# Down projection: the next chunk's weight loads queued behind the fifth product's token operands, and a 384-byte filler in phase one

## The chip, the cores and the metric

The kernel runs on one core of one Trainium2 chip. A core has TensorE (PE in the profile, with PEld for its weight loads), VectorE (DVE), ScalarE (ACT), GpSimd (POOL) and SyncE (SP), which here issues nearly all DMA transfers. Each engine runs its own instruction list in order. The metric is the device time of one execution in microseconds (us).

## The reference

A trunk of two layers on 1024 tokens of width 1024, in float32. Each layer computes

```
h = rms_norm(x, attn_norm[l])
proj = h @ w_in[l]                  # 1312 columns, shared by three mixers
mixed = concat(sliding-window attention, pooling mixer, latent attention)
x = x + mixed @ w_out[l]
h = rms_norm(x, ffn_norm[l])
x = x + (silu(h @ w_gate[l]) * (h @ w_up[l])) @ w_down[l]    # width 2816
```

The change concerns the last product of the last line, and the memory layout of the first product.

## The kernel before

Every float32 product is made of three TensorE passes: each operand is split into a rounded part and a remainder (`split`, line 58: a ScalarE copy, then a VectorE subtraction), and the passes are high by high, high by low and low by high.

A layer has these parts. **Phase one** (`phase1`) makes the input projection, the windowed attention and the pooling mixer, 128 tokens at a time. **Phase two** (`phase2`) makes the latent attention and the output projection. `gate_up` makes the gate and up products and their gated product; `down` makes the down projection.

Both feed-forward halves use a seven-product scheme for 2 by 2 blocks (Winograd's form of Strassen's), so each block product takes seven multiplications and a number of additions. `gate_up` works on eleven column pairs. For each pair its generator `operands` forms seven combinations of the gated product, splits each of them and stores the two parts in DRAM, in `gd[i][0]` to `gd[i][6]` (line 1278). The stores of the last pair are left to the generator in `G["kept"]`, which `down` drives on.

**The down projection.** The eleven pairs are taken in four chunks of 2, 3, 3 and 3 pairs. For a chunk of h pairs, `load` (line 1026) brings 2h blocks of `w_down`, 512 KB each, into a tile `rw`. Chunk one has a buffer of its own; chunks two, three and four use the pool `even`, which has two buffers, so that chunk four takes the one that chunk two had. `chunk` then makes seven products in the order 1, 2, 5, 6, 3, 7, 4. For each product, `operands(at, p, b)` does two things:

- it loads the token operand, h transfers of 512 KB from `gd` into a tile `ga` (line 1041); the pool `sg` has four `ga` buffers, so the operand of the fifth product can be loaded only when the first product is done;
- it splits the weight operand `q[b]` into a tile `op` (ACT line 1043, DVE line 1044); the pool `sw` has three buffers. Between them `sub` (POOL line 1034) forms sums of weights in place in `rw`.

Each product then takes four groups of 3h matmuls (lines 1085 to 1087), one group for each 128 token rows, with a sum in PSUM (`acc`), which ACT (line 1090) or DVE (`add`, line 1075) moves to the accumulators `a1`, `a5`, `a6` and `xrow`. In chunk one, `rows` reloads the residual rows `xrow` from DRAM (line 1050) and drives `G["kept"]`.

**What sets the order.** The text gives priorities; a scheduler then fixes each engine's instruction list before the run, by simulating a timeline: among the instructions that are ready in that simulation it takes the one that stands earlier in the text. On the chip the lists are run as they are, and every instruction waits for the semaphores of its inputs and of the buffers that it overwrites. `tc.issue_after(ins)` places what is traced in its block behind `ins` on the same engine's list; it adds no wait for `ins` to end.

In the text, the loads of the next chunk (`ahead()`) stand behind the third product's operands.

**Phase one's layout.** Pools take SBUF in the order in which they are opened. `gap` opens a pool that only takes room, and writes one element of it on POOL (line 52) so that the pool exists. Two such gaps, of 1024 and 2176 bytes for each partition, stand in `phase1`. The pools `wt` (the first 512 columns of the projection's weights, `wa`) and `wz` (a part of the other columns, `wb`) are the last ones.

Of the kernel before, what the change touches and what calls it, by code (L numbers as in the profile page):

```python
# [21 lines left out]
P = 128  # L22
# [14 lines left out]
def trunk(ctx: ExitStack, tc: tile.TileContext, A, out):  # L37
# [62 lines left out]
    for l in range(DEPTH):  # L100
        xsrc = A["x"][0] if l == 0 else xres
        G = dict(
            ident=ident, xm=xm, xrow=xrow, krr=krr, rc=rc, cosT=cosT, sinT=sinT, sinks=sinks,
            pscale=pscale, invc=invc, nhalf=nhalf, gq=gq, gm=gm, cmask=cmask, identr=identr, rn=rn, gc=gc, g32=g32, xsrc=xsrc, dram=dram, gap=gap, xp=xp, gns=ExitStack(), bias_keep=bias_keep)
        G["gna"], G["gains"], G["gqk"] = gna, gains, gqk
        phase1(nc, tc, A, l, pool, split, f, bcast, G)
        phase2(nc, tc, A, l, pool, split, f, bcast, G)
        phase34(nc, tc, A, l, pool, split, f, bcast, G, xres, out)
# [217 lines left out]
def phase1(nc, tc, A, l, pool, split, f, bcast, G):  # L326
    ve, sc, gp, te, sy = nc.vector, nc.scalar, nc.gpsimd, nc.tensor, nc.sync
    cosT, sinT = G["cosT"], G["sinT"]
    ident, xm, xrow, krr = G["ident"], G["xm"], G["xrow"], G["krr"]
    with ExitStack() as ph:  # L330
        gap = G["gap"]
# [14 lines left out]
        hp = [pool(ph, f"p1h_{l}"), hq]  # L346
        early = pool(ph, f"p1e_{l}")
        wj = pool(ph, f"p1j_{l}")
        wt = pool(ph, f"p1t_{l}")
        wz = pool(ph, f"p1z_{l}")  # L350
        ps_mm = pool(ph, f"p1mm_{l}", bufs=2, space=PSUM)
# [21 lines left out]
        hTs, rows = {}, {}  # L373
        behind = []
        ahead = {}
# [60 lines left out]
        for t in range(NT):  # L436
# [3 lines left out]
            hT, r = hTs[t], rows[t]  # L440
# [149 lines left out]
            for g in range(2):  # L590
# [3 lines left out]
                for i0, ni in ((0, 2), (2, 1)):  # L594
                    s = ps_sc.tile([P, 2, 256], F32, name="s")
                    for i in range(i0, i0 + ni):
                        h = 3 * g + i
# [6 lines left out]
                for i in range(3):  # L604
                    h = 3 * g + i
# [3 lines left out]
                for i in range(3):  # L609
                    h = 3 * g + i  # L610
# [373 lines left out]
def phase34(nc, tc, A, l, pool, split, f, bcast, G, xres, out):  # L984
    ve, sc, gp, te, sy = nc.vector, nc.scalar, nc.gpsimd, nc.tensor, nc.sync
    ident, xm, xrow, xp = G["ident"], G["xm"], G["xrow"], G["xp"][l]
    last = l == DEPTH - 1
    HB = S // 2
    HK = KT // 2
    gd = [[G["dram"].tile([P, 2, HB], F32, name=f"gd{l}_{i}_{p}") for p in range(7)] for i in range(NF // 2)]  # L990

    with ExitStack() as ph:
        ps_gu = pool(ph, f"p4gu_{l}", bufs=5, space=PSUM)
        ps_d = pool(ph, f"p4dn_{l}", bufs=3, space=PSUM)
        gate_up(nc, tc, A, l, pool, split, f, bcast, G, ps_gu, ps_d, gd)
        G["gns"].close()

        down(nc, tc, A, l, pool, split, f, G, (ps_gu, ps_d), gd, xres, out)


def down(nc, tc, A, l, pool, split, f, G, banks, gd, xres, out):

    ve, sc, gp, te, sy = nc.vector, nc.scalar, nc.gpsimd, nc.tensor, nc.sync
    xrow, xp = G["xrow"], G["xp"][l]
    last = l == DEPTH - 1
    LEFT, RIGHT = slice(0, 512), slice(512, 1024)
    with ExitStack() as ph:  # L1010
        sg = pool(ph, f"p5s_{l}", bufs=4)
        ac = pool(ph, f"p5a_{l}")
        a1 = ac.tile([P, 4, 512], F32, name="a1")
        a5 = ac.tile([P, 4, 512], F32, name="a5")
        a6 = ac.tile([P, 4, 512], F32, name="a6")
        even = pool(ph, f"p5e_{l}", bufs=2)
        G["go"] = pool(ph, f"p5g_{l}", bufs=2)
        sw = pool(ph, f"p5w_{l}", bufs=3, side="right")

        def load(ps, rp):  # L1020
            h = len(ps)
            rw = rp.tile([P, 2 * h, D], F32, name="rw")
            for b in range(2):
                for j, i in enumerate(ps):
                    r = (2 * i + b) * P
                    sy.dma_start(rw[:, b * h + j], A["w_down"][l, r : r + P, :])
            q = {f"B{a + 1}{b + 1}": rw[:, a * h : a * h + h, c] for a in range(2) for b, c in enumerate((LEFT, RIGHT))}
            return ps, q, h

        def chunk(loaded, first, final, ahead=None):  # L1030
            ps, q, h = loaded

            def sub(o, a, b):
                gp.tensor_tensor(out=o, in0=a, in1=b, op=ALU.subtract)  # L1034

            ops, nxt = {}, []

            def operands(at, p, b):
                ga = sg.tile([P, 3, 2, 512], F32R, name="ga")
                for j, i in enumerate(ps):  # L1040
                    sy.dma_start(f(ga[:, j]), gd[i][at])
                t = sw.tile([P, 2, 3, 512], F32R, name="op")[:, :, 0:h]
                sc.copy(t[:, 0], q[b])  # L1043
                ve.tensor_tensor(out=t[:, 1], in0=q[b], in1=f(t[:, 0]), op=ALU.subtract)  # L1044
                ops[p] = ga, t

            def rows(ts, n):
                if first:
                    for t in ts:
                        sy.dma_start(xrow[t], xp[t])  # L1050
                    for _ in range(n):
                        next(G["kept"], None)

            operands(0, 1, "B11")
            operands(1, 2, "B21")
            rows(range(4), 0)
            sub(q["B12"], q["B12"], q["B11"])
            operands(2, 5, "B12")
            rows(range(4, 6), 7)
            if ahead is not None:  # L1060
                nxt.append(ahead())
            sub(q["B12"], q["B22"], q["B12"])
            operands(3, 6, "B12")
            rows(range(6, 8), 0)
            if first:
                for t in range(4, NT):
                    gp.tensor_tensor(out=xrow[t][:, LEFT], in0=xrow[t][:, LEFT], in1=xrow[t][:, RIGHT], op=ALU.subtract)
            sub(q["B11"], q["B12"], q["B11"])
            sub(q["B21"], q["B21"], q["B12"])
            operands(4, 3, "B22")  # L1070
            operands(5, 7, "B11")
            operands(6, 4, "B21")

            def add(o, a, eng=ve):
                eng.tensor_tensor(out=o, in0=o, in1=a, op=ALU.add)

            for at, p in enumerate((1, 2, 5, 6, 3, 7, 4)):
                S_, T_ = ops[p]
                for i in range(4):
                    lo, hi = xrow[i], xrow[i + 4]  # L1080
                    n = 4 * at + i
                    acc = banks[n % 8 > 4].tile([P, 512], F32, name="dn", tag=("gu", "dn")[n % 8 > 4])
                    ts = slice(i * P, (i + 1) * P)
                    for j in range(h):
                        te.matmul(acc, S_[:, j, 0, ts], T_[:, 0, j], start=j == 0, stop=False)  # L1085
                        te.matmul(acc, S_[:, j, 0, ts], T_[:, 1, j], start=False, stop=False)  # L1086
                        te.matmul(acc, S_[:, j, 1, ts], T_[:, 0, j], start=False, stop=j == h - 1)  # L1087
                    dst = (a1[:, i], lo[:, LEFT], lo[:, RIGHT], hi[:, LEFT], a5[:, i], a6[:, i], hi[:, RIGHT])[p - 1]
                    if first and p in (1, 5, 6):
                        sc.copy(dst, acc)  # L1090
                    else:
                        add(dst, acc)
                    if not final:
                        continue
                    if p == 1:
                        add(lo[:, LEFT], a1[:, i], gp)
                    elif p == 6:
                        add(a6[:, i], a1[:, i], gp)
                        add(hi[:, LEFT], a6[:, i], gp)
                        add(a5[:, i], a6[:, i], ve)  # L1100
                        add(lo[:, RIGHT], a5[:, i], ve)
                    elif p == 7:
                        add(hi[:, LEFT], hi[:, RIGHT], ve)
                        add(hi[:, RIGHT], a5[:, i], ve)
                    if p in (3, 4):
                        t = i if p == 3 else i + 4
                        dst = out[0] if last else xres
                        sy.dma_start(dst[t * P : (t + 1) * P, :], xrow[t])
            return nxt

        with ExitStack() as st:
            first = load(range(0, 2), pool(st, f"p5z_{l}", side="right"))
            nxt = chunk(first, True, False, lambda: load(range(2, 5), even))
        nxt = chunk(nxt[0], False, False, lambda: load(range(5, 8), even))
        nxt = chunk(nxt[0], False, False, lambda: load(range(8, 11), even))
        chunk(nxt[0], False, True)


# [271 lines left out]
```

## Time and profile before

| | |
|---|---|
| median of 3 runs | 2178.31 us (2177.22 to 2181.81) |
| profiled execution | 2177.97 us |
| its span, first to last instruction | 2176.1 us |
| mean granted TensorE clock | 0.990 |
| down projection, layer 0, on PE | 874.4 to about 1091 us |
| down projection, layer 1, on PE | 1956.1 to about 2171 us |

Times in the views are in us from the span's start. A row of the timeline gives the start, the length, the engine, the line, the operation, the tiles as output<-input, and the count; what stands in brackets is how long the engine was idle before it, and what released it. On SP a row counts issues of transfers, whose data land later. In a view of stretches, `PE busy (x)` is the busy time and the number of instructions that lie in the stretch, PEclk is the clock that was granted, DMA share the share of the sixteen DMA engines' time, and GB/s what they moved.

### The profile page before, as it was taken

Reading aid. Unit: us, or ns where it says so; the run is one execution under the profiler, and the core shown is the slowest. Engines: PE = TensorE matmul, PEld = TensorE weight load, DVE = VectorE, ACT = ScalarE, POOL = GpSimd, SP = SyncE. Lnnn points to the kernel's source line nnn. Section 1 sums busy time; section 2 is a strip of 40 time slices with the busy share of each in tenths; the row PEclk is TensorE's granted clock in tenths of the full one; section 3 lists DMA queues with packets and bytes.
Section 4 is the critical chain, followed back from the end, with each engine's and each line's share of the span. In section 5 each row is a group of like instructions: output and inputs, shape, how many; then the busy total and the mean of one; then the engine's idle time right before and its main releaser. Section 6 shows DMA issues by size and latency. Waiting matters only on the chain.

```text
span 2176.1 us, 29696 instructions
## 1 busy us (share of the span) xinstructions
PE 2096.3 (96%) x10423; PEld 1756.8 (81%) x10423; DVE 1689.1 (78%) x2595; ACT 1084.4 (50%) x2301; POOL 976.0 (45%) x916
## 2 busy tenths in 40 slices
PE   8998999999999999999989989999999999999999
PEld 6886898877888888788878868888778888887887
DVE  6567888799888887765756678887998878877657
ACT  7777676663434333321267777766534443333111
POOL 2445456256544452522624354552654545436215
PEclk9999999999999999999999999999999999999999
DMA  7002211324445335975530122113144344369754
GB/s 232 1 1 97 92 45 49 117 87 145 164 144 176 136 136 194 411 300 196 204 105 1 37 93 83 49 59 128 69 158 169 138 156 151 140 229 406 272 200 164
DMA packets 133732, 312.16 MB, mean 143 GB/s; under 512 B 13071, under 2 KB 63952, under 8 KB 133584
## 3 DMA queue, kind: packets, MB, share of 16 engines
q1 hardware_dynamic: 133396, 310.19, 39.8%
q8 instruction: 83, 1.36, 0.2%
q14 instruction: 65, 0.53, 0.1%
q10 hardware_dynamic: 188, 0.08, 0.0%
HBM read 203.53 MB, written 106.70 MB: 143 GB/s over the span
## 4 chain that ended last, share of the span: by engine, by line
PE 45%; DVE 7%; DMA 5%; issue 2%; ACT 2%; POOL 1%; SPq 0%; DVEq 0%; ACTq 0%; POOLq 0%
PE dn L1085 5%; PE dn L1086 5%; PE dn L1087 5%; PE gu L1240 5%; PE gu L1239 5%; PE gu L1238 5%; PE acc L446 2%; PE acc L447 2%; PE acc L448 2%; DMA ga<-gd 1%; DMA rw<-in_w_down_dram 1%; PE tp L847 1%; PE po L888 1%; PE po L886 1%; PE po L887 1%
## 5 line engine op out<-in xcount | busy, mean ns | idle before, releaser
L1240 PE MATMUL gu<-T,sb 128*128 128x512 f32 x704 | 274.8, 391 | 9.0 <-DVE sb L58 8.8
L1238 PE MATMUL gu<-T,sb 128*128 128x512 f32 x704 | 274.9, 390 | 4.9 <-DVE B L58 2.0
L1239 PE MATMUL gu<-T,sb 128*128 128x512 f32 x704 | 274.0, 389 | 0.0
L1085 PE MATMUL dn<-op,ga 128*128 128x512 f32 x616 | 240.6, 392 | 8.5 <-DMA ga<-gd 8.5
L1086 PE MATMUL dn<-op,ga 128*128 128x512 f32 x616 | 240.7, 391 | 0.0
L1087 PE MATMUL dn<-op,ga 128*128 128x512 f32 x616 | 239.9, 391 | 0.0
L58 ACT CAST go<-xm 128x512 fp32r<-128x512 f32 x154 | 94.8, 620 | 264.5 <-POOL xm L1272 98.6
L1034 POOL TENSOR_TENSOR rw<-rw 128x1536 f32<-128x1536 f32 (+1 forms) x32 | 110.9, 3477 | 245.3 <-DVE op L1044 156.3
L1043 ACT CAST op<-rw 128x1536 fp32r<-128x1536 f32 (+1 forms) x56 | 76.9, 1376 | 284.9 <-PE dn L1087 266.6
L1215 POOL TENSOR_TENSOR xm<-raw 128x512 f32<-128x512 f32 x44 | 68.1, 1550 | 322.3 <-DMA raw<-in_w_up_dram 110.5
L58 DVE TENSOR_TENSOR go<-xm,go 128x512 fp32r<-128x512 f32 x154 | 155.8, 1021 | 34.2 <-ACT go L58 30.1
L58 ACT CAST sb<-raw 128x512 fp32r<-128x512 f32 x180 | 110.1, 617 | 118.0 <-PE gu L1240 97.2
L1240 PEld LDWEIGHTS gu<-T,sb 128*128 128x128 f32 x704 | 132.1, 188 | 40.4 <-DVE sb L58 13.1
L1238 PEld LDWEIGHTS gu<-T,sb 128*128 128x128 f32 x704 | 132.1, 188 | 35.2 <-ACT sb L58 3.5
L58 DVE TENSOR_TENSOR sb<-raw,sb 128x512 fp32r<-128x512 f32 x180 | 157.2, 874 | 1.3 <-ACT sb L58 0.3
L1272 POOL TENSOR_TENSOR xm<-xm 128x512 f32<-128x512 f32 x88 | 142.6, 1628 | 30.1 <-DVE go L58 19.3
L1239 PEld LDWEIGHTS gu<-T,sb 128*128 128x128 f32 x704 | 132.2, 188 | 27.2
L1044 DVE TENSOR_TENSOR op<-rw,op 128x1536 fp32r<-128x1536 f32 (+1 forms) x56 | 114.4, 2044 | 39.1 <-ACT op L1043 36.1
L1085 PEld LDWEIGHTS dn<-op,ga 128*128 128x128 f32 x616 | 116.4, 189 | 34.5 <-issue 7.3
L1087 PEld LDWEIGHTS dn<-op,ga 128*128 128x128 f32 x616 | 116.2, 189 | 24.6
L1086 PEld LDWEIGHTS dn<-op,ga 128*128 128x128 f32 x616 | 116.5, 189 | 24.0
L1238 PE MATMUL gu<-B,A 128*128 128x512 f32 x336 | 131.5, 391 | 2.8 <-ACT B L58 2.8
(332 smaller groups left out, 6071.4 us busy)
## 6 DMA issues: line engine op xcount, KB each, us to landing
gd<-go SPq DMA_DIRECT2D x154, 512.0 KB, 3.1
ga<-gd SPq DMA_DIRECT2D x154, 512.0 KB, 5.9
raw<-in_w_gate_dram SPq DMA_DIRECT2D x22, 1024.0 KB, 5.6
raw<-in_w_up_dram SPq DMA_DIRECT2D x22, 1024.0 KB, 6.2
rw<-in_w_down_dram SPq DMA_DIRECT2D x44, 512.0 KB, 8.7
xp<-stage SPq DMA_DIRECT2D x32, 256.0 KB, 2.0
old<-xp SPq DMA_DIRECT2D x16, 512.0 KB, 4.2
xp<-xm SPq DMA_DIRECT2D x16, 512.0 KB, 2.9
```

Source lines behind the costliest of these rows:

```text
L58: return sc.copy(hi, src), ve.tensor_tensor(out=lo, in0=src, in1=f(hi), op=ALU.subtract)
L1034: gp.tensor_tensor(out=o, in0=a, in1=b, op=ALU.subtract)
L1043: sc.copy(t[:, 0], q[b])
L1044: ve.tensor_tensor(out=t[:, 1], in0=q[b], in1=f(t[:, 0]), op=ALU.subtract)
L1085: te.matmul(acc, S_[:, j, 0, ts], T_[:, 0, j], start=j == 0, stop=False)
L1086: te.matmul(acc, S_[:, j, 0, ts], T_[:, 1, j], start=False, stop=False)
L1087: te.matmul(acc, S_[:, j, 1, ts], T_[:, 0, j], start=False, stop=j == h - 1)
L1215: gp.tensor_tensor(out=s1, in0=q["A21"], in1=q["A22"], op=ALU.add)
L1238: te.matmul(acc, s[:, 0, k], b[:, 0, k], start=k == 0, stop=False)
L1239: te.matmul(acc, s[:, 0, k], b[:, 1, k], start=False, stop=False)
L1240: te.matmul(acc, s[:, 1, k], b[:, 0, k], start=False, stop=k == HK - 1)
L1272: gp.tensor_tensor(out=q[o], in0=q[a], in1=q[b], op=op)
```

## The change

The loads of a chunk get a `pin`: an earlier issue on SP behind which they are queued, one behind the other. `operands` keeps its last `ga` transfer in `pin`. The loads for the next chunk move in the text from behind the third product's operands (`operands(2, 5, ...)`) to behind those of the fifth (`operands(4, 3, ...)`), and are pinned to the last of that operand's transfers. The step `rows(range(4, 6), 7)`, which loads two residual rows and drives the seven kept stores, moves behind the fourth product's operands. This holds for the first three chunks; the fourth has nothing to load ahead. In `phase1`, a third gap of 384 bytes stands ahead of `wt`.

```diff
+        gap(ph, f"p1m_{l}", 384)
         wt = pool(ph, f"p1t_{l}")
         wz = pool(ph, f"p1z_{l}")
...
-        def load(ps, rp):
+        def load(ps, rp, pin=None):
             h = len(ps)
             rw = rp.tile([P, 2 * h, D], F32, name="rw")
             for b in range(2):
                 for j, i in enumerate(ps):
                     r = (2 * i + b) * P
-                    sy.dma_start(rw[:, b * h + j], A["w_down"][l, r : r + P, :])
+                    with tc.issue_after(pin.ins) if pin else nullcontext():
+                        pin = sy.dma_start(rw[:, b * h + j], A["w_down"][l, r : r + P, :])
...
             ops, nxt = {}, []
+            pin = []
 
             def operands(at, p, b):
                 ga = sg.tile([P, 3, 2, 512], F32R, name="ga")
                 for j, i in enumerate(ps):
-                    sy.dma_start(f(ga[:, j]), gd[i][at])
+                    pin[:] = [sy.dma_start(f(ga[:, j]), gd[i][at])]
...
             operands(2, 5, "B12")
-            rows(range(4, 6), 7)
-            if ahead is not None:
-                nxt.append(ahead())
             sub(q["B12"], q["B22"], q["B12"])
             operands(3, 6, "B12")
+            rows(range(4, 6), 7)
             rows(range(6, 8), 0)
...
             operands(4, 3, "B22")
+            if ahead is not None:
+                nxt.append(ahead(pin[0]))
             operands(5, 7, "B11")
...
-            nxt = chunk(first, True, False, lambda: load(range(2, 5), even))
-        nxt = chunk(nxt[0], False, False, lambda: load(range(5, 8), even))
-        nxt = chunk(nxt[0], False, False, lambda: load(range(8, 11), even))
+            nxt = chunk(first, True, False, lambda pin: load(range(2, 5), even, pin))
+        nxt = chunk(nxt[0], False, False, lambda pin: load(range(5, 8), even, pin))
+        nxt = chunk(nxt[0], False, False, lambda pin: load(range(8, 11), even, pin))
```

## The prediction, made before the changed kernel had run

> **What bounds the kernel now.** I read the page's head first, then stretches of the down projection, then TensorE's waits, then its timeline and SP's.
>
> ```profile
> PE 2096.3 (96%) x10423; PEld 1756.8 (81%) x10423; DVE 1689.1 (78%) x2595; ACT 1084.4 (50%) x2301; POOL 976.0 (45%) x916
> ```
>
> TensorE is busy for 2096.3 of 2176.1 us. Time can be won only where PE waits or runs at a lower clock; a faster helper elsewhere wins nothing.
>
> ```profile
> 874.00:919.00 45.00, 40.24 (x170) 32.32 (x169) 35.81 (x30) 16.54 (x24) 26.31 (x11) 0.96 1.03 411
> 1956.00:2001.00 45.00, 41.29 (x174) 33.34 (x174) 33.83 (x27) 17.59 (x25) 25.70 (x11) 0.96 1.02 410
> 919.00:1091.00 172.00, 171.93 (x759) 142.04 (x757) 114.18 (x130) 36.60 (x32) 62.95 (x26) 1.00 0.65 237
> 2001.00:2171.00 170.00, 170.00 (x752) 140.76 (x751) 111.60 (x123) 27.96 (x20) 62.35 (x24) 1.00 0.60 222
> ```
>
> The columns are length, then PE, PEld, DVE, ACT and POOL busy, PEclk, DMA share, GB/s. The first two rows are chunk one of each layer: PE lacks 4.76 and 3.71 us, its clock is 0.96, and the DMA engines are full (1.03 and 1.02) at 411 GB/s. The last two rows are the other three chunks: PE is full, so nothing is to be won there.
>
> ```profile
> PE dn L1085 <- DMA ga<-gd: 8.5, 4, 3.3
> ```
>
> All of the down projection's waits on PE are for token operands: 8.5 us in four waits, two in each layer.
>
> ```profile
> 874.37 0.39 PE L1085 MATMUL dn<-op,ga 128*128 128x512 f32 x1
> 879.81 0.39 PE L1085 MATMUL dn<-op,ga 128*128 128x512 f32 x1
> 897.99 0.47 PE L1085 MATMUL dn<-op,ga 128*128 128x512 f32 x1 [1.49 <-DMA ga<-gd]
> 906.95 0.76 PE L1085 MATMUL dn<-op,ga 128*128 128x512 f32 x1 [3.27 <-DMA ga<-gd]
> 907.51 0.63 PE L1086 MATMUL dn<-op,ga 128*128 128x512 f32 x1
> 907.94 0.63 PE L1087 MATMUL dn<-op,ga 128*128 128x512 f32 x1
> 919.41 0.39 PE L1085 MATMUL dn<-op,ga 128*128 128x512 f32 x1
> ...
> 1956.05 0.39 PE L1085 MATMUL dn<-op,ga 128*128 128x512 f32 x1
> 1978.45 0.47 PE L1085 MATMUL dn<-op,ga 128*128 128x512 f32 x1 [0.48 <-DMA ga<-gd]
> 1987.41 0.47 PE L1085 MATMUL dn<-op,ga 128*128 128x512 f32 x1 [3.23 <-DMA ga<-gd]
> 2000.04 0.39 PE L1085 MATMUL dn<-op,ga 128*128 128x512 f32 x1
> ```
>
> Rows one and two are the first matmuls of products one and two: a product of chunk one takes 879.81 - 874.37 = 5.44 us, or 0.227 us for each of its 24 matmuls. The waits stand where the fifth and the sixth product begin. After the long one the starts lie 0.43 us apart (907.51, 907.94), so PE runs at about half speed for a while: each long wait costs more than itself. The whole price is the length of the chunk. Seven products at 5.44 are 38.08 us. Layer 0's chunk took 919.41 - 874.37 = 45.04 us, layer 1's 2000.04 - 1956.05 = 43.99 us. **Lost: 6.96 and 5.91, together 12.87 us.**
>
> Why the operands come late is in SP's order (layer 0) and in the chain of waits:
>
> ```profile
> 876.82 0.32 SPq L1050 DMA_DIRECT2D xm<-xp  x1
> 877.25 1.31 SPq L1026 DMA_DIRECT2D rw<-in_w_down_dram  x3
> 880.04 0.33 SPq L1050 DMA_DIRECT2D xm<-xp  x1
> 881.18 0.33 SPq L1278 DMA_DIRECT2D gd<-go  x1
> 883.99 0.32 SPq L1050 DMA_DIRECT2D xm<-xp  x1
> 884.36 0.99 SPq L1026 DMA_DIRECT2D rw<-in_w_down_dram  x2
> 886.81 0.33 SPq L1278 DMA_DIRECT2D gd<-go  x1
> 887.18 1.28 SPq L1026 DMA_DIRECT2D rw<-in_w_down_dram  x2
> 888.56 0.89 SPq L1041 DMA_DIRECT2D ga<-gd  x2
> 890.26 5.38 SPq L1026 DMA_DIRECT2D rw<-in_w_down_dram  x5
> 896.64 2.88 SPq L1041 DMA_DIRECT2D ga<-gd  x3
> ```
>
> ```profile
> 888.02 8.55 DMA rw<-in_w_down_dram
> 896.64 10.18 DMA ga<-gd
> ...
> 1977.10 10.18 DMA ga<-gd
> ```
>
> Twelve weight loads (3+2+2+5) are issued here, which is chunk two's six and chunk three's six, since `even` has two buffers. Seven stand ahead of the fifth product's two operands, all twelve ahead of the sixth's. Every transfer is 512 KB: 524,288 bytes at 411 GB/s are 1.276 us. Counting rows, the fifth's first operand is transfer 13, the sixth's first is transfer 20. It landed at 896.64 + 10.18 = 906.82, and PE went on at 906.95. Counted back, transfer n lands at 906.82 - 20 x 1.276 + 1.276n = 881.30 + 1.276n. Test: transfer 13 gives 897.89, and PE went on at 897.99. So this stretch is a line of transfers at a fixed rate, and only the place in the line matters.
>
> **The change, part by part.**
>
> *The pins in chunk one.* Only chunk two's six loads are left in this line; chunk three's are pinned behind chunk two's fifth operands. The fifth operands' buffer comes free when product one ends, at 879.81 + 0.39 = 880.2, so they go out as transfers 2 and 3, and land by about 881.30 + 3 x 1.276 = 885.1; they are needed at 874.37 + 4 x 5.44 = 896.1. The waits of 1.49 and 0.48 go. For the sixth I take the worst order, with all that stood ahead before and six loads fewer: 6 x 1.276 = 7.66 us earlier, 899.2 in layer 0 and 1977.10 + 10.18 - 7.66 = 1979.6 in layer 1. PE, no longer held up, needs them at 874.37 + 5 x 5.44 = 901.6 and at 1956.05 + 27.2 = 1983.3. Both long waits go, with margins of 2.4 and 3.7 us, and the half-speed stretches with them. What is late next? The seventh's operands stand right behind, two transfers or 2.6 us later, and are needed 5.44 later.
>
> *Chunk two's weights.* In the worst order above, the six loads are transfers 4 to 13 with the others among them: landed by 881.30 + 13 x 1.276 = 897.9, before by 896.6.
>
> ```profile
> 890.13 3.52 POOL L1034 TENSOR_TENSOR rw<-rw 128x1536 f32<-128x1536 f32 x1
> ...
> 903.72 1.47 ACT L1043 CAST op<-rw 128x1536 fp32r<-128x1536 f32 x1 [5.65 <-PE dn L1087]
> ```
>
> Their first user is POOL's sum at 890.13, which may start some 5 us later; it serves chunk two's third product, 16 us after that chunk's start. The first cast, at 903.72, was released by PE (an `op` buffer), not by the weights. It can start at 901.6 in the new time, 3.7 us after the landing. Cost: 0.
>
> *Chunks three and four.* A product takes 9 x 4 x 0.227 = 8.16 us there. The chunk's fifth operands go out one product after its start, then the six loads: nine transfers, 11.5 us, so landed some 20 us after its start. The next chunk's first cast can begin after five products, 40.8 us. Cover: 21 us. The room on the DMA engines is there:
>
> ```profile
> 931.00:960.00 29.00, 29.00 (x130) 24.01 (x129) 21.76 (x23) 4.64 (x4) 6.66 (x3) 1.00 0.65 235
> 975.00:1045.00 70.00, 70.00 (x311) 57.95 (x310) 38.30 (x43) 13.36 (x9) 19.80 (x8) 1.00 0.57 200
> ```
>
> At shares of 0.65 and 0.57 the moved 7.7 us fit, and the operands loaded behind them have four buffers, over 20 us, in hand. Cost: 0.
>
> *The new place in SP's list.* SP stands at the fifth operands until 880.2, with the loads, residual rows and kept stores queued behind. The transfers already issued keep the DMA engines busy until 881.3, so about nothing is lost. The `rows` step, now later, drives stores that only chunk four reads. Cost: 0.
>
> *The gap.* Two more memsets on POOL:
>
> ```profile
> L52 POOL MEMSET gap<- x4: 96/98/99, 0.9 to 1092.9; 128x1 f32 x4
> ```
>
> That is 0.2 us on an engine that is idle for over half of the span. The shift of `wt` and `wz` by 384 bytes can change which buffers wait for which at the passage from phase one to two, and the scheduler may then order those phases otherwise. The trace doesn't show this. The nearest rows are the second phases of both layers:
>
> ```profile
> 168.00:442.00 274.00, 256.31 (x1537) 223.50 (x1536) 221.09 (x469) 189.27 (x458) 130.32 (x148) 0.96 0.25 84
> 1258.00:1524.00 266.00, 248.25 (x1521) 216.58 (x1519) 218.56 (x465) 185.94 (x455) 128.48 (x148) 0.98 0.24 81
> ```
>
> PE lacks 17.69 and 17.75 us. The layers already lie differently in phase one (the `raw` buffers are eleven and five), yet lose the same; so I take 0, and keep ends of half such a loss, 8.9 us, either way.
>
> **Sum.** 12.87 less some 0.2 us that layer 0 loses ahead of the first wait, for which no operand is the cause: 12.6 us. The profiled execution took 2177.97 us (its span of 2176.1 and 1.9 around it), and comes to 2165.4. The median of the three runs is 0.3 higher: 2178.31 - 12.6 = **2165.7 us**.
>
> **The rivals.**
>
> *The sixth product still waits.* If SP puts three more transfers ahead of its operands (kept stores, residual rows), they come 3.8 us later, and with a margin of 2.4 us layer 0 waits 1.4 us; with a bubble at the new stand on SP, some 3. The Trainium skill ("DMA: Bandwidth & Descriptors", section "Anatomy of one DMA — SWDGE (gpsimd) path") speaks for such a bubble: DMA engines don't wait on semaphores, the issuing sequencer does, and a transfer has about 2.0 us of fixed cost (fitted there on another issuing path than SP's; no row here separates it). By that, the fifth operands' data start only at 882.2, 0.9 us after the line ran dry, an estimate; the sum stays the same as long as the margin holds. A wait of 3 us brings half speed with it: the long wait of layer 0 cost 906.95 to 919.41, 12.46 us for two products of 10.88, so 1.6 us more. Both layers at 3 + 1.6 would leave 9 of 12.6: 2175; layer 0 alone 2170.3. I price it at 2171. Against it: the count above was the worst order already.
>
> *It doesn't do what it says.* The DMA engines are full in chunk one, and if the scheduler fills the freed places with other transfers, chunk two's operands among them, the waits stay and the time is 2178. Against it: those need `ga` buffers that come free only with later products.
>
> *Slower: phase two's order is dealt anew.* The gap changes buffer waits at the passage to phase two; if one layer's order there loses twice its 17.7 us, the time is 2165.7 + 17.7 = 2183.4. It decides from 12.6 us on, and shows beyond the measurement (0.2%, 4.4 us, is what can be told from no change) from 17.0. For it: these phases are where PE's lost time is. Against it: the two layers' equal losses. A lucky deal, half of the loss gone, gives 2157 to 2162.
>
> **How the numbers follow.** Forecast 0.60, the sixth still waits 0.14, lucky deal 0.07: faster 0.81. Nothing gained, or a deal that eats the gain: same 0.10. Slower 0.09. The range takes in the forecast, the late sixth and part of the lucky deal: 2159 to 2174. It leaves out the last two cases, about 2 in 10.
>
> **What would show it.** On SP, two `ga` issues come ahead of the first `rw` in chunk one, six `rw` there instead of twelve, and six in each of chunks two and three. The chunk-one stretches shrink from 45.0 and 44.0 us to 38 with PEclk 1.00, and the group of PE waits for `ga` is gone. The stretch behind them keeps its 171.9 and 170.0 us. Wrong would be: a wait of `dn` for `op`, ACT or POOL waiting for `rw` with PE behind them, or phases one and two of another length than before (874.4 us to layer 0's down projection, 865 us from its end to layer 1's).

## The result, and the profile after

| | before | after |
|---|---|---|
| median | 2179.56 us (2177.22 to 2181.81, 4 runs) | 2168.27 us (2162.74 to 2168.79, 4 runs) |
| ratio of the times | | 0.9945, 95% interval 0.9931 to 0.9959 |
| profiled execution | 2177.97 us | 2168.79 us |
| its span | 2176.1 us | 2167.0 us |

The change makes the kernel faster by 0.55%, or 11.3 us between the medians. The forecast was 2165.7 us.

The page's first part after, TensorE's row:

```profile
PE 2095.3 (97%) x10423; PEld 1757.3 (81%) x10423; DVE 1690.8 (78%) x2595; ACT 1085.5 (50%) x2301; POOL 978.2 (45%) x918
```

PE is busy as long as before (2095.3 against 2096.3 us); the span around it is shorter. POOL has two instructions more, which are the two memsets of the gap. The stretches of the down projection after, in the prediction's columns:

```profile
874.00:912.00 38.00, 37.70 (x166) 30.71 (x166) 35.23 (x30) 16.53 (x24) 21.89 (x10) 1.00 0.97 365
1951.20:1989.20 38.00, 38.00 (x170) 31.45 (x169) 31.03 (x28) 16.94 (x24) 21.91 (x10) 1.00 0.99 382
912.00:1086.00 174.00, 173.72 (x767) 143.57 (x765) 116.88 (x131) 36.70 (x32) 67.98 (x28) 1.00 0.70 263
1989.20:2161.00 171.80, 171.80 (x760) 142.25 (x759) 114.48 (x125) 28.82 (x20) 67.29 (x25) 1.00 0.65 246
```

The first two rows lie over chunk one of each layer. The clock there is 1.00 instead of 0.96, PE lacks 0.30 and 0.00 us instead of 4.76 and 3.71, and the DMA engines move 365 and 382 GB/s instead of 411 and 410. The last two rows are the other chunks: PE is still full, and the moved loads show as a DMA share of 0.70 and 0.65 instead of 0.65 and 0.60. What is left of the waits of `dn` for `ga`, in the view of TensorE's waits after:

```profile
PE dn L1088 <- DMA ga<-gd: 0.3, 1, 0.3
```

One wait of 0.3 us stands where four with 8.5 us stood. TensorE's timeline after, at the first matmuls of product one, five and six of layer 0's chunk one, of its chunk two, and of the same chunks in layer 1:

```profile
875.42 0.39 PE L1088 MATMUL dn<-op,ga 128*128 128x512 f32 x1
897.18 0.39 PE L1088 MATMUL dn<-op,ga 128*128 128x512 f32 x1
903.09 0.47 PE L1088 MATMUL dn<-op,ga 128*128 128x512 f32 x1 [0.30 <-DMA ga<-gd]
914.20 0.39 PE L1088 MATMUL dn<-op,ga 128*128 128x512 f32 x1
...
1952.86 0.39 PE L1088 MATMUL dn<-op,ga 128*128 128x512 f32 x1
1990.94 0.39 PE L1088 MATMUL dn<-op,ga 128*128 128x512 f32 x1
```

Chunk one takes 914.20 - 875.42 = 38.78 us in layer 0 and 1990.94 - 1952.86 = 38.08 in layer 1. Product five begins on time (897.18 - 875.42 = 4 x 5.44). Product six begins late by 903.09 - 897.18 - 5.44 = 0.47 us. Cut at the first matmuls of each stage in the same timelines, both spans add up as follows (us; layer 0's down projection is counted to 0.22 us, one spacing, after its last matmul starts):

| stage on PE | before | after | after less before |
|---|---|---|---|
| start, and phases one and two, layer 0 | 442.27 | 442.59 | +0.32 |
| gate and up, layer 0 | 432.10 | 432.83 | +0.73 |
| **chunk one, layer 0** | 45.04 | 38.78 | **-6.26** |
| other chunks, layer 0 | 171.36 | 171.36 | 0.00 |
| passage, and phases one and two, layer 1 | 433.72 | 434.52 | +0.80 |
| gate and up, layer 1 | 431.56 | 432.78 | +1.22 |
| **chunk one, layer 1** | 43.99 | 38.08 | **-5.91** |
| other chunks and the end, layer 1 | 176.07 | 176.07 | 0.00 |

The two chunks give 12.17 us, the other stages take 3.07 back, and 9.10 us are left between the spans of these two executions. The sections below ask which part of the change gives the 12.17, and whether it also causes the 3.07.

### The profile page after: what moved, and what is told of

Same layout as the page of the kernel before. It is cut to its first block, busy times and chain, and to the rows that moved or that the text cites. A ratio compares the mean times of both kernels' runs of the same rounds, so it can differ in the third digit from the quotient of the medians.

```text
span 2167.0 us, 29690 instructions
## 1 busy us (share of the span) xinstructions
PE 2095.3 (97%) x10423; PEld 1757.3 (81%) x10423; DVE 1690.8 (78%) x2595; ACT 1085.5 (50%) x2301; POOL 978.2 (45%) x918
## 4 chain that ended last, share of the span: by engine, by line
PE 47%; DVE 7%; DMA 4%; issue 2%; ACT 1%; POOL 1%; SPq 0%; DVEq 0%; ACTq 0%; POOLq 0%
PE dn L1088 6%; PE dn L1090 6%; PE dn L1089 6%; PE gu L1243 5%; PE gu L1242 5%; PE gu L1241 5%; PE acc L448 2%; PE acc L449 2%; PE acc L447 2%; DMA ga<-gd 1%; PE tp L848 1%; PE po L889 1%; PE po L887 1%; PE po L888 1%; DMA raw<-in_w_up_dram 1%
```

## The experiments

Each ran beside the kernel before on the same chip, and its ratio is to those runs of before. Lengths of stages are of each run's one profiled execution, cut as above; "phases, layer 1" is the stretch from the last product of layer 0 to layer 1's gate and up.

| kernel | median us | ratio to before, 95% | chunk one, layer 0 / 1 | phases, layer 1 |
|---|---|---|---|---|
| before | | | 45.04 / 43.99 | 433.72 |
| after | 2168.27 | 0.9945 (0.9931 to 0.9959) | 38.78 / 38.08 | 434.52 |
| rows_back | 2165.37 | 0.9931 (0.9918 to 0.9945) | 40.03 / 38.08 | 434.64 |
| no_gap | 2167.72 | 0.9939 (0.9928 to 0.9951) | 39.52 / 38.08 | 436.32 |
| gap_only | 2178.62 | 0.9990 (0.9978 to 1.0002) | 46.05 / 44.14 | 433.60 |
| text_only | 2178.43 | 0.9994 (0.9983 to 1.0006) | 46.00 / 44.05 | 434.70 |
| count_only | 2165.51 | 0.9938 (0.9923 to 0.9953) | 38.48 / 38.08 | 436.45 |
| order_only | 2180.92 | 1.0003 (0.9994 to 1.0012) | 46.76 / 47.19 | 429.36 |
| three_more | 2180.49 | 1.0003 (0.9991 to 1.0015) | 43.25 / 42.15 | 438.33 |
| rows_last | 2174.15 | 0.9967 (0.9954 to 0.9980) | 38.51 / 38.08 | 439.71 |
| behind_fourth | 2166.12 | 0.9945 (0.9932 to 0.9957) | 38.08 / 38.08 | 434.73 |
| behind_second | 2175.73 | 0.9986 (0.9977 to 0.9995) | 38.51 / 38.08 | 440.40 |

### The gap and the place of `rows`

gap_only is before with the gap alone:

```diff
+        gap(ph, f"p1m_{l}", 384)
         wt = pool(ph, f"p1t_{l}")
```

> The kernel before with the 384-byte gap and nothing else. Line theory: time as before within 1.5 us, chunk one about 45 and 44 us. Rival (the gap carries a part of the gain, or costs one): median over 3 us from the kernel before, with the difference in phases one and two.

no_gap is after without that line:

> The changed kernel without the 384-byte gap. Line theory: time as the changed kernel within 1 us, chunk one 38.1 to 38.8 us. Rival (the shifted buffers change waits in phases one and two): phase one and two of layer 1 differ by over 1.5 us from the changed kernel's 162.05 and 267.80 us in the same direction in the median, and the median by over 2 us.

rows_back is after with the two residual rows and the seven kept stores in their old place:

```diff
             operands(2, 5, "B12")
+            rows(range(4, 6), 7)
             sub(q["B12"], q["B22"], q["B12"])
             operands(3, 6, "B12")
-            rows(range(4, 6), 7)
```

> The changed kernel with the step rows(range(4, 6), 7) back at its old place in the text. Line theory (what counts in chunk one is the place of the token operands in the line of transfers): the step decides nothing, time as the changed kernel, 2163 to 2169 us, ratio to before 0.994 to 0.995, chunk one 38.1 to 38.8 us in both layers. Rival (the later stores are a part of the gain): over 2 us slower than the changed kernel.

gap_only can't be told from before, and no_gap and rows_back can't be told from after: the intervals overlap. The instruction lists of the built programs say why. Those of gap_only differ from before's by the two memsets alone, and so do no_gap's from after's; rows_back's are the same as after's on every engine. So the gap and the place of `rows` in the text do nothing here, and rows_back and no_gap are further samples of after. Their chunk one in layer 0 took 40.03 and 39.52 us, more than the 38.1 to 38.8 expected and 1.25 and 0.74 more than after's, which is the size of what chance moves between executions of one list. It is the sixth product that is late each time. In rows_back the view puts its wait of 1.55 us down to a cast on ACT, but that cast makes chunk two's first operand; the product's own token operand, issued at 890.76, landed 11.73 us later, 0.14 us before the product began at 902.63.

### Where the gain comes from

text_only is after with the loads in their new place in the text, but not pinned:

```diff
             if ahead is not None:
-                nxt.append(ahead(pin[0]))
+                nxt.append(ahead(None))
```

> The changed kernel's text order with the pins of the loads on the token operands left out (the loads keep their order among themselves). SP then issues seven loads ahead of the fifth's operands and twelve ahead of the sixth's, as before. Line theory: chunk one 44 to 45 us in both layers, median 2177 to 2181: the pins are the change. Rival (the place in the text is enough): chunk one under 40, median under 2170.

count_only leaves chunk two's loads in their old place, unpinned; those of chunks three and four stay pinned. So the line of chunk one has six loads, but they stand ahead of the fifth operands as before:

```diff
             operands(2, 5, "B12")
+            if ahead is not None and (first):
+                nxt.append(ahead(None))
...
-            if ahead is not None:
+            if ahead is not None and not (first):
                 nxt.append(ahead(pin[0]))
```

> Chunk two's loads where they stood before, unpinned, so ahead of the fifth product's operands; chunk three's and four's loads as in the change. Only six loads instead of twelve are left in chunk one, and SP issues one row, six loads, two rows, two stores, then the fifth's operands. Line theory: the fifth's operands are transfer 11, the sixth's 13 instead of 20; the sixth's wait goes, the fifth waits 0 to 1.5 us; chunk one 38.1 to 40.5 us, median within 3 us of the changed kernel. Rival (the fifth's operands must stand ahead of the weights): both waits stay, chunk one 42 to 45 us, median 2175 or more.

order_only is the other half: chunk two's loads are pinned behind the fifth operands, those of chunks three and four stand in their old place, unpinned:

```diff
             operands(2, 5, "B12")
+            if ahead is not None and (not first):
+                nxt.append(ahead(None))
...
-            if ahead is not None:
+            if ahead is not None and not (not first):
                 nxt.append(ahead(pin[0]))
```

> Chunk two's loads behind the fifth product's operands as in the change; chunk three's loads back where they stood, unpinned. SP issues the fifth's operands, nine loads, then the sixth's, then three more loads. Line theory: the fifth doesn't wait; the sixth's operands are three transfers (3.8 us) later than in the changed kernel, where they had no margin in layer 0 (a wait of 0.3) and about 1 us in layer 1, so waits of 3 to 4 and 2 to 3 us, with 1.5 us of half speed where they are long: chunk one 41 to 44.5 us, median 2173 to 2178. Rival (the order alone carries the gain): chunk one under 39.5, median under 2171.

The waits of `dn` for `ga` on TensorE (us in total, times, longest), first text_only:

```profile
PE dn L1088 <- DMA ga<-gd: 8.4, 4, 3.3
```

then count_only:

```profile
PE dn L1090 <- DMA ga<-gd: 0.2, 1, 0.2
```

then order_only:

```profile
PE dn L1090 <- DMA ga<-gd: 12.7, 4, 4.0
```

In text_only the waits are those of before, and SP's order in the down projection is that of before: the scheduler left the loads where they were though they stand later in the text, so it is the pin that moves them. count_only has the whole gain though its loads stand ahead of the fifth operands. order_only has no gain: SP puts nine loads between the fifth and the sixth operands, and three more ahead of the seventh. SP's timeline of order_only (start, length, number of issues; the data land later):

```profile
886.15 1.22 SPq L1044 DMA_DIRECT2D ga<-gd  x2
887.42 6.02 SPq L1028 DMA_DIRECT2D rw<-in_w_down_dram  x9
894.44 1.56 SPq L1044 DMA_DIRECT2D ga<-gd  x2
896.95 0.33 SPq L1028 DMA_DIRECT2D rw<-in_w_down_dram  x1
...
899.51 1.61 SPq L1028 DMA_DIRECT2D rw<-in_w_down_dram  x2
```

Its waits are longer than before's. The expectation counted the sixth product alone; the seventh waits too, for 3.50 us in layer 0 and 3.99 in layer 1. So each chunk one came out longer than the 41 to 44.5 us that were expected, and longer than before's: the order in which the fifth operands go first even costs something when all twelve loads follow. Layer 1's phases, at 429.36 us 4.4 shorter than before's, hide this in the span. So **what the gain needs is six loads fewer in the line, and that is done by the pin in chunk two**, which keeps chunk three's loads out of chunk one. The pin in chunk one, by which the change is described, adds nothing that these runs can tell.

### The line of transfers, tested by lengthening it

three_more is after with three more 512 KB transfers, from the weights to a place in DRAM that nobody reads, between the fifth operands and the six loads of chunk one:

```diff
             operands(4, 3, "B22")
+            if first:
+                for n in range(3):
+                    spare = G["dram"].tile([P, D], F32, name=f"spare{l}{n}")
+                    with tc.issue_after(pin[0].ins):
+                        pin[:] = [sy.dma_start(spare, A["w_down"][l, (2 * 2 + n) * P : (2 * 2 + n + 1) * P, :])]
```

> The changed kernel with three more transfers of 512 KB in chunk one of each layer, weight rows copied to a DRAM tile that nothing reads, behind the fifth's operands and ahead of chunk two's loads. Line theory at 1.276 us for each transfer: the sixth's operands come 3.8 us later; layer 0 had nothing to spare (waits of 0.3 to 1.7), so it waits 4 to 5.5 us, chunk one 43 to 46 us with the half-speed time; layer 1 had some 1.9 us to spare, so it waits about 2, chunk one 40 to 42. Rival (the DMA engines have room, since they ran at a share of 0.6 to 0.9 there): chunk one under 40 in both.

TensorE's waits in three_more:

```profile
PE dn L1093 <- DMA ga<-gd: 5.7, 2, 3.5
```

The waits are back at the sixth product, 3.5 us in layer 0 and 5.7 - 3.5 = 2.2 in layer 1. Three transfers are 3 x 1.276 = 3.83 us in the prediction's line. So layer 1 had 3.83 - 2.2 = 1.6 us to spare in after, and layer 0 next to nothing. The chunks grew by 4.47 and 4.07 us, more than the waits, since half speed came back behind them: in layer 1 matmuls start 0.43 us apart behind the wait (1990.03 and 1990.46, for instance) instead of 0.23. The line holds, and after stands at its edge. The median of three_more says less, since its phases in layer 1 took 438.33 us, which has a cause of its own (below).

### Why the sixth operands have no margin

The prediction gave them 2.4 us. SP's timeline after, in layer 0's chunk one:

```profile
877.55 3.54 SPq L1053 DMA_DIRECT2D xm<-xp  x2
881.89 0.32 SPq L1281 DMA_DIRECT2D gd<-go  x1
884.70 0.32 SPq L1053 DMA_DIRECT2D xm<-xp  x1
887.51 0.32 SPq L1281 DMA_DIRECT2D gd<-go  x1
887.92 1.20 SPq L1044 DMA_DIRECT2D ga<-gd  x2
889.17 3.23 SPq L1028 DMA_DIRECT2D rw<-in_w_down_dram  x6
892.75 1.56 SPq L1044 DMA_DIRECT2D ga<-gd  x2
```

The fifth operands (the fifth row) went out at 887.92. Their buffer came free when product one ended, counted as in the prediction at 875.42 + 5.44 + 0.39 = 881.25. Until then and for 6.67 us more SP stood at residual rows (`xm<-xp`) and kept stores (`gd<-go`). The chain of waits after says what those waited for (start, length, what; rows under 0.1 us are left out):

```profile
880.75 1.11 DVE go L58
881.86 2.81 DVE xm L1300
884.70 0.63 ACT go L58
885.35 2.14 DVE go L58
887.51 0.32 SPq L1281
...
887.92 4.77 DMA ga<-gd
892.75 10.20 DMA ga<-gd
```

DVE makes the last token operands of gate and up (`xm`, `go`), SP stores them, and the fifth operands are queued behind those stores. The weight loads that used to stand between the rows and stores kept the DMA engines busy in this time. Now they stand behind the fifth operands, and the engines run partly dry, as the stretches of after show (DMA share and GB/s at the end of each row):

```profile
884.00:886.00 2.00, 2.00 (x10) 1.65 (x9) 1.31 (x2) 1.30 (x3) 2.00 (x2) 1.00 0.82 246
886.00:888.00 2.00, 2.00 (x11) 1.65 (x10) 2.00 (x2) 2.00 (x4) 2.00 (x2) 1.00 0.64 221
888.00:890.00 2.00, 2.00 (x11) 1.65 (x10) 2.00 (x2) 1.69 (x3) 1.92 (x2) 1.00 0.89 274
```

Before, the middle one of these stretches had 1.02 and 410 GB/s:

```profile
886.00:888.00 2.00, 2.00 (x11) 1.65 (x10) 2.00 (x2) 2.00 (x4) 1.95 (x2) 1.00 1.02 410
```

From there on the line runs at its known rate: the sixth operands, behind the six loads, landed 10.20 us after their issue, which is 8 x 1.276 (six loads and two operands). They landed at 892.75 + 10.20 = 902.95, and were needed at 875.42 + 5 x 5.44 = 902.62. The prediction's worst order is the order that came: the sixth's first operand is the fourteenth transfer, due at 899.16, or 900.21 with this chunk's start 1.05 us later. It landed 2.74 us after that, which is what the dry stretch cost.

rows_last was made to win this time back. It queues the last residual rows and the kept stores behind chunk two's loads:

```diff
             operands(3, 6, "B12")
-            rows(range(4, 6), 7)
-            rows(range(6, 8), 0)
...
             if ahead is not None:
-                nxt.append(ahead(pin[0]))
+                nxt.append(ahead(pin))
+            with tc.issue_after(pin[0].ins):
+                rows(range(4, 6), 7)
+                rows(range(6, 8), 0)
...
```

Here `load` leaves its last issue in `pin`, and POOL's subtraction on these residual rows moves with them.

> The changed kernel with the later residual rows and the kept stores queued on SP behind chunk two's last load, so that SP no longer stands at them while the DMA engines run dry. Line theory: the fifth's operands go out as the second transfer, the six loads right behind; the sixth's land some 2 us ahead of their use in layer 0; no wait in chunk one, 38.1 us in both layers, 0.7 to 1.9 us less in layer 0 than with the change; median within 3 us of the changed kernel, since phases one and two of layer 1 get another order. Rival (SP's stand at the stores only moves): layer 0 still waits 0.5 us or more.

The fifth operands went out at 880.51 there, but chunk one in layer 0 still took 38.51 us instead of the 38.1 expected. The two rows and two stores now stand between the six loads and the sixth operands, which landed 0.2 us late. Nor did the median stay within 3 us of after's: it is 5.9 us higher, and its interval only touches after's and lies above those of rows_back and no_gap. The lost time lies elsewhere: the phases of layer 1 took 439.71 us against 434.52 in after.

### The order dealt to layer 1's phases

The scheduler fixes the lists of layer 1's phases after it has placed layer 0's down projection, and what is changed there changes their order. PE's list has 2410 instructions in this stretch. It is the same in before, gap_only and text_only, another in after, no_gap and rows_back, and a third in rows_last. In the traces three_more's is rows_last's but for three instructions. Two kernels place only chunk three's loads in layer 0 anew; their chunk one is after's. behind_fourth puts them behind chunk two's fourth operands:

```diff
             operands(3, 6, "B12")
+            if ahead is not None and (l, ps[0]) in [(0, 2)]:
+                nxt.append(ahead(pin[0]))
...
-            if ahead is not None:
+            if ahead is not None and (l, ps[0]) not in [(0, 2)]:
                 nxt.append(ahead(pin[0]))
```

> After, with one place changed: in layer 0's second chunk, the six loads of the third chunk's weights stand behind the fourth product's operands instead of the fifth's. Chunk one's order on SP is after's (six loads ahead of the sixth operands). PE's list for layer 1's phases one and two is that of order_only in all but 5 of 2410 instructions, and unlike after's in some 1070 of them. Theory A (the order that the scheduler deals to layer 1's phases decides their length): the stretch from layer 0's last product to layer 1's gate and up takes about 429.4 us, as in order_only, against 434.5 in after; chunk one 38 to 39 us in both layers, the rest of the chunks 171.4: about 2163 us, some 5 below after. Theory B (order_only's short phases came from something else, such as the later end of its chunk one or one lucky execution): 434.5 us there, about 2168 us in all.

behind_second puts them behind chunk two's second operands (`operands(1, 2, "B21")`), by the same edit at that place:

> After, with one place changed: in layer 0's second chunk, the six loads of the third chunk's weights stand behind the second product's operands. Chunk one's order on SP is after's. PE's list for layer 1's phases one and two is that of rows_last, whose stretch there took 439.7 us. Theory A (the dealt order decides): about 439.7 us again, 5 above after, about 2173 us in all, though chunk one takes 38 to 39 us in both layers. Theory B (rows_last lost its 5 us through its late stores and residual rows, or by chance): 434.5 us there, about 2168 us.

The stretch in rows_last (length, then PE busy, as above):

```profile
1085.40:1525.10 439.70, 409.04 (x2412) 354.88 (x2411) 321.91 (x668) 302.18 (x770) 190.27 (x283) 0.98 0.21 69
```

and in behind_second:

```profile
1086.40:1526.80 440.40, 410.09 (x2411) 356.62 (x2410) 322.74 (x668) 302.23 (x770) 188.66 (x283) 0.97 0.21 69
```

and in after:

```profile
1085.60:1520.10 434.50, 407.48 (x2412) 353.70 (x2411) 322.70 (x668) 304.03 (x770) 187.82 (x283) 0.98 0.21 70
```

behind_second bears theory A out: with the list of rows_last and none of its moved rows and stores, it has that kernel's 440 us. Its median is 7.5 us above after's. Of the 6.2 us between the two spans 5.9 lie here, and 2.9 went with a wait of PE for DVE in layer 0's chunk two; the other stages differ by 2.6 the other way. Together with three_more, the kernels with this list or nearly this list took 438.3 to 440.4 us here, and the three with after's list 434.5 to 436.3. So rows_last lost this time with its dealt order, and not by its late stores. The rows also say how. Length less PE busy is PE's idle time: 30.7 and 30.3 us in rows_last and behind_second, 27.0 in after, and by the same view 27.1 in rows_back and 27.0 in no_gap. The rest of the difference is busy time, which also varies within one list: 407.5, 407.5 and 409.3 us in after, rows_back and no_gap.

behind_fourth is a miss. Phases one and two of layer 1, first in order_only:

```profile
1092.30:1253.50 161.20, 154.51 (x881) 133.96 (x881) 97.92 (x197) 117.36 (x315) 58.00 (x135) 0.98 0.14 47
1253.50:1521.60 268.10, 251.94 (x1532) 219.86 (x1531) 221.42 (x471) 188.15 (x456) 131.01 (x148) 0.98 0.25 84
```

then in behind_fourth:

```profile
1084.50:1246.20 161.70, 154.90 (x881) 134.06 (x881) 97.85 (x197) 117.24 (x315) 58.36 (x135) 0.98 0.14 47
1246.20:1519.20 273.00, 256.37 (x1534) 223.75 (x1532) 221.66 (x472) 188.23 (x456) 130.75 (x148) 0.96 0.25 83
```

Phase one came out as short as expected (161.7 and 161.2 us with the passage, against 166.7 in after), but phase two took 4.9 us longer, at a clock of 0.96 instead of 0.98, with PE longer busy by 4.43 us on the same work. Over both rows PE's idle time is 22.9 us in order_only and 23.4 in behind_fourth, against 27.0 in after. So the dealt order brought the shorter waits again, and a longer busy time took the gain back. Whether that comes of the few instructions that differ or of chance stays open. Its median of 2166.12 us can't be told from after's. No version was found that beats after by more than the measurement can tell: rows_back, count_only and behind_fourth lie 2 to 3 us below its median, inside the intervals.

## Why the prediction was right, point by point

**What bounds the kernel, and the price of chunk one: right.** The loss was put at 12.87 us and the gain at 12.6; chunk one gave 6.26 + 5.91 = 12.17. Layer 1 reached the full 38.08 us. The stretches behind it kept their length: 171.36 us for the other chunks of layer 0, and 176.07 in layer 1 with the end of the span. So chunks two to four paid nothing for the moved loads.

**The line of transfers: right.** The rate of 1.276 us held in after (10.20 us for eight), and in three_more the three added transfers of 3.83 us gave waits of 3.5 and 2.2 us.

**Fewer loads or another order: the reason was right.** The step credits "the pins in chunk one" but counts six loads less, and the count is what works: count_only has all of it, order_only none.

**The new place in SP's list: mis-sized.** This is the step that did not hold: "SP stands at the fifth operands until 880.2 ... so about nothing is lost", and the fifth operands "land by about ... 885.1". The buffer was not what SP waited for last. Residual rows and kept stores, which wait for DVE, stand ahead in its list; the fifth operands went out at 887.92 and landed at 887.92 + 4.77 = 892.69. That is before they were needed (897.18), but it pushed the sixth: margins given as 2.4 and 3.7 us were -0.3 and about 1.6. The bubble that the rival "the sixth product still waits" spoke of is there, with a cause one step earlier. Its price in layer 0 was 0.7 us in after (38.78 - 38.08), 1.44 in no_gap and 1.95 in rows_back, instead of 3 and more. The step puts rows and stores behind the fifth operands, and in the list they stand ahead. The worst order for the sixth was right in its count; what the step left out is the 2.74 us by which the line came late. The margin of 2.4 us was not made for this, and that it nearly covered it was luck. SP's timeline of before showed the stores waiting between the weight loads; the loads that filled those waits are the ones that the change takes away. The rival's other premise, that a wait of 3 us brings half speed with it, is no rule either: order_only's sixth product in layer 0 went on at full speed after 3.24 us.

**The other zeros.** `rows` and the gap cost nothing, as forecast. What the gap was feared for happened by another way: the edit in the down projection itself deals layer 1's phases anew. In the kernels here that stretch took between 429.4 and 440.4 us; the bound of 8.9 us either way covers this, and after's order came out 0.8 us longer than before's, less than the 1.8 us by which three kernels with after's list differ.

**The 3.07 us given back.** The prediction named phases of another length as a sign of being wrong: its 874.4 us to layer 0's down projection became 875.4, and its 865 from there to layer 1's became 867.3. Of this, gate and up took 0.73 and 1.22 us more, though the lists of these stages are the same in both kernels. These stretches before, then after:

```profile
442.20:874.30 432.10, 424.83 (x1872) 348.47 (x1873) 369.65 (x451) 182.40 (x320) 211.40 (x136) 1.00 0.42 148
1524.50:1956.00 431.50, 424.87 (x1872) 348.46 (x1873) 371.94 (x455) 182.52 (x319) 210.69 (x136) 1.00 0.42 150
```

```profile
442.60:875.40 432.80, 426.46 (x1872) 349.70 (x1873) 373.91 (x452) 182.85 (x319) 211.19 (x135) 1.00 0.42 148
1520.10:1952.80 432.70, 425.12 (x1872) 348.36 (x1873) 369.40 (x455) 182.46 (x319) 211.35 (x136) 1.00 0.42 149
```

Kernels with the old chunk one show the same spread (gap_only 433.29 and 431.74, text_only 432.32 and 432.66), so two single executions can differ by this without the change. For the phases (0.32 and 0.80 us) the spread within one list is 1.8 us, as above, so a part due to the change is not shown. The medians, 11.3 us apart, lie nearer to the 12.17 than the spans do; rows_back, a further sample of after, is 14.2 us below its own runs of before. The forecast of 2165.7 us is 2.6 us under the measured median and inside the spread of after's runs.

## What to carry to other kernels

When transfers queue in one line at a fixed rate, count what stands ahead of the operand that is waited for, and ask which of it is needed only later: taking six loads out of the line gave all of the gain, and reordering the line alone gave none. Before you move a transfer back on its queue, look at what its neighbours on that queue wait for, since the transfer may have been what kept the DMA engines busy during their waits. An edit that changes a scheduler's timeline deals the stages behind it anew; here one such order went with 4 to 6 us, up to half the gain, in three kernels, so compare stage by stage before you credit a time to the edit.

## What the runs showed of the hardware that was not expected

The same wait doesn't always bring half speed. TensorE's timeline of order_only, in phase two of layer 1:

```profile
1337.04 0.44 PE L848 MATMUL tp<-ident,Pt 128*128 128x128 f32 x2 [1.20 <-POOL Pt L840]
1337.23 0.48 PE L887 MATMUL po<-wo,mh 128*128 128x512 f32 x1
1337.55 0.40 PE L888 MATMUL po<-wo,mh 128*128 128x512 f32 x1
1337.79 0.28 PE L821 MATMUL ss<-kT,qT 96*128 96x256 f32 x1
```

The same place in behind_fourth:

```profile
1329.74 0.69 PE L848 MATMUL tp<-ident,Pt 128*128 128x128 f32 x2 [1.20 <-POOL Pt L840]
1330.08 0.78 PE L887 MATMUL po<-wo,mh 128*128 128x512 f32 x1
1330.65 0.63 PE L888 MATMUL po<-wo,mh 128*128 128x512 f32 x1
1331.08 0.41 PE L821 MATMUL ss<-kT,qT 96*128 96x256 f32 x1
```

Both waited 1.20 us for the same tile. In order_only the next product began 1337.79 - 1337.55 = 0.24 us later, in behind_fourth 1331.08 - 1330.65 = 0.43. Longer waits are no surer. Those of 3.27 and 3.23 us in chunk one brought half speed in both layers of before, and so did one of 2.19 us in layer 1 of three_more. But in layer 0 of order_only, TensorE ran on at full speed after a wait of 3.24 us in the same place:

```profile
904.75 0.47 PE L1090 MATMUL dn<-op,ga 128*128 128x512 f32 x1 [3.24 <-DMA ga<-gd]
905.05 0.40 PE L1091 MATMUL dn<-op,ga 128*128 128x512 f32 x1
```

Here 905.05 - 904.75 = 0.30 us, and the starts that follow lie 0.23 apart. What decides was not found. It may be why PE's busy time varies between executions of one list, but no run here tests that.
